# Conv-out products moved to the end of a merge stage, conv taps spread over ten attention rounds, and eight modulation chunks computed on VectorE

## The chip, the cores and the metric

The kernel runs on one NeuronCore of a Trainium2 chip. The metric is the device time of one execution in microseconds (us); of the kernel before it is the median of three runs. The trace quoted here is of one further execution taken by the hardware profiler.

The engines are named as in the profile: PE is TensorE (PEld its weight loads), DVE is VectorE, ACT is ScalarE, POOL is GpSimd, and SP is SyncE, which here only issues DMAs. PEclk is the clock granted to TensorE as a share of full speed: 1.00 is its upper level, 0.50 its lower one.

## What is computed

Two transformer blocks on 512 tokens of width 1024, in float32. The change lies in the first block:

```python
mod = silu(c) @ ada_w + ada_b                       # 1024 -> 6 x 1024: sh1 sc1 ga1 sh2 sc2 ga2
h = rmsnorm(x, pre_mix_g) * (1 + sc1) + sh1
glu_in, qkv, gates = split(h @ w_in)
u = silu(layernorm(depthwise_conv31(u_val * sigmoid(u_gate))))
y_conv = u @ w_conv_out                             # "cout"
y_att = stick_breaking_attention(q, k, v) @ w_att_out   # 8 heads; "aout"
merged = sigmoid(g_conv) * y_conv + sigmoid(g_att) * y_att
y = merged @ w_o                                    # "wo"
x = x + ga1 * rmsnorm(y, post_mix_g)                # needs ga1
h = rmsnorm(x, pre_ffn_g) * (1 + sc2) + sh2         # needs sc2, sh2: the second modulation
x = x + ga2 * rmsnorm(swiglu_ffn(h), post_ffn_g)
```

The second block (retention, latent attention, a conv feed-forward) is not touched.

## The kernel before

**Products.** Every float32 product is done as three float32r products (`mm3`, lines 202 to 204) of split operands: hi x hi, lo x hi, hi x lo. A weight slab of 512 KB is loaded by SP into a `w_st` buffer (a ring of 2), cast by ACT into `w_hi` (line 184), and its remainder is computed into `w_lo` by DVE or POOL (line 207); `w_hi` and `w_lo` have four buffers each. `slab()` takes the next slab of the fixed list `ORDER` and issues slabs ahead.

**Order.** The program is written in one order, and a planner in the framework orders the queue of each engine: it gives each instruction a due time by its own costs, and where several are ready it takes the one that is earliest in the program. On the chip each engine then follows its queue in order. Buffers of one tag are handed out in the order of the program: a tile waits until the tile that is as many back as the tag has buffers is released.

**PSUM.** There are eight banks: two in `psT` (given out by `pt()`, tile `ps_t`), four in `psP` (`pp()`, tile `ps_p`), two in `psC` (tile `ps_c`). The conv accumulators hold `psC` until the taps are done; then `Banks.both` is set and `pp()` uses `psC` as well.

**Attention rounds.** `pipeline` runs ten rounds, t = 0 to 9. In round t head t computes scores and the scan (lines 712 to 723), head t-1 transposes its weights (228), head t-2 multiplies by v (679) and combines (702). `stick_between(t)` then adds the fillers of `STICK_FILL`: q and k products, gate products (16 tiles of 24 products), and before the change `cout` 0 and 1. `step(conv, n)` advances the generator `conv_all` by n parts: fifteen parts of two taps of each of the four channel tiles (three on DVE, line 523; the fourth by ACT and POOL, lines 526 and 527), a last tap with the layer norm of the first token tile, three more layer norms, and the transposes back with SiLU. Three parts are advanced before round 0.

**Modulation chunks.** `ada_acc` computes one chunk of 256 columns of `mod`: two half tiles `ad` of 512 KB each are loaded (line 360). On PE it is sixteen short matmuls (line 385) and a DVE copy (390). On DVE (`ADA.vector`) it is one multiply (376) and seven multiply-adds (378) into the single buffer `acc`. Either way a small PE product over `acc` follows, in a `psT` bank: line 396 for the sc2/sh2 columns (`ada_cols`, then DVE 400 and 403), line 416 for a quarter of the row of ga1 (`ga_row`, then DVE 417 and 418 into `grow`). In the merge the pool `mtmp` has two `ad` buffers, which are the two halves of one chunk, and one `acc` buffer.

**Merge.** For p = 0 to 3: the two remaining conv gates (p >= 2) and `cout` p, then `aout` p; DVE multiplies by the gates (lines 772 and 847), POOL adds (848), ACT casts and DVE subtracts into `mh` and `ml_` (849, 850). Chunks 0 to 5 of the second modulation are done on PE in rounds 3 to 8; chunks 6 and 7 and the four rows of ga1 on DVE in the merge.

**After the merge** the `wo` product runs through `gemm_tok` with eight slabs: four are streamed over all four token tiles, four are resident. The accumulators of its first token tile are the two `psT` banks, those of the others `pp()` banks. `boundary` then updates x with `grow1` (line 331) and makes the next h.

Of the kernel before, what the change touches and what calls it, by code (L numbers as in the profile page):

```python
# [8 lines left out]
F32 = mybir.dt.float32  # L9
# [9 lines left out]
S = 512  # L19
KB = 8  # L20
# [29 lines left out]
for _n, _k in VEC:  # L50
# [6 lines left out]
ORDER = (  # L57
    [("glu", k) for k in range(8)]
    + [("win", 3), ("win", 7)]
    + [("v", i) for i in range(4)]  # L60
)
def _fill(spec):
    return tuple(
        [({"q": "q", "k": "k", "g": "gate", "c": "cout"}[x[0]], int(x[1:])) for x in r.split()] for r in spec.split("|")
    )


STICK_FILL = _fill("q1 k1|g8|q2 k2|g9|q3 k3|g10 g11|g12 g13|g14 g15|g0 g1 c0|g2 g3 c1")
WIN_OF = {"q": 8, "k": 12}
ORDER += [("win", 8), ("win", 12)]  # L70
for _f in STICK_FILL:
    ORDER += [("win", WIN_OF[n] + m) if n in WIN_OF else (n, m) for n, m in _f]
for _p in range(4):
    if _p >= 2:
        ORDER += [("gate", 2 * _p), ("gate", 2 * _p + 1), ("cout", _p)]
    ORDER += [("aout", _p)]
ORDER += [("wo", k) for k in range(8)]
for _m in range(NF):
    ORDER += [("fin", _m), ("fin", NF + _m)]
# [16 lines left out]
def build(tc, nc, a):  # L96
# [38 lines left out]
    def pp():  # L135
        Banks.at = (Banks.at + 1) % 6
        if Banks.both and Banks.at % 3 == 0:
            return conv_bank()
        ps_p = psP.tile([128, 512], F32, tag="p", name="ps_p")
        return ps_p  # L140
# [23 lines left out]
    def vcol(name, i):  # L164
        o = VOFF[name] + i
        return vec[:, o:o + 1]
# [26 lines left out]
    def slab(key, ahead=2):  # L193
        assert ORDER[W.got] == key, (ORDER[W.got], key)
        W.got += 1
        if W.nxt < W.got:
            emit_slab()
        prefetch(ahead)
        return W.ready.pop(key)
# [16 lines left out]
    def mtile(ps, w, rh, rl, nk, width, c0=0, t0=0, t1=S):  # L216
        wh, wl = w
        for k in range(nk):
            c = k * width + c0
            mm3(  # L220
                ps[:, t0:t1], wh[:, c:c + 128], wl[:, c:c + 128],
                rh[:, k, t0:t1], rl[:, k, t0:t1], k == 0, k == nk - 1,
            )
# [128 lines left out]
    class ADA:  # L352
        pool, tag, bufs, nacc = ring, "st", NST, 1
# [10 lines left out]
    def ada_acc(chunk, ap_):  # L364

        ads = ADA.loaded.pop(chunk, None) or ada_load(chunk)
        if ADA.vector:  # L370
            acc = ap_.tile([128, 256], F32, tag="acc", name="acc", bufs=ADA.nacc)
            for hf, ad in enumerate(ads):
                for b in range(4):
                    cc = cact[:, 4 * hf + b, 0:1]
                    if hf == 0 and b == 0:
                        nc.vector.tensor_scalar(out=acc, in0=ad[:, b, :], scalar1=cc, scalar2=None, op0=ALU.mult)
                    else:
                        nc.vector.scalar_tensor_tensor(
                            out=acc, in0=ad[:, b, :], scalar=cc, in1=acc, op0=ALU.mult, op1=ALU.add
                        )  # L380
            return acc, pt()[:, 256:512]
        ps = pt()
        for hf, ad in enumerate(ads):
            for b in range(4):
                nc.tensor.matmul(  # L385
                    out=ps[32 * b:32 * b + 32, 0:256], lhsT=cact[:, 4 * hf + b, :], rhs=ad[:, b, :],
                    start=hf == 0, stop=hf == 1,
                )
        acc = ap_.tile([128, 256], F32, tag="acc", name="acc", bufs=ADA.nacc)
        nc.vector.tensor_copy(acc, ps[:, 0:256])  # L390
        return acc, ps[:, 256:512]

    def ada_cols(i, kb, g_name, ap_):
        acc, ps = ada_acc(8 * i + kb, ap_)
        for s in range(2):
            nc.tensor.matmul(
                out=ps[:, s:s + 1], lhsT=acc[:, s * 128:(s + 1) * 128], rhs=ones[:, 0:1], start=True, stop=True
            )
        sh, sc = 24 * i + kb, 24 * i + 8 + kb
        nc.vector.tensor_tensor(  # L400
            out=modB[:, i, kb:kb + 1], in0=ps[:, 0:1], in1=vcol("ada_b", sh), op=ALU.add
        )
        nc.vector.scalar_tensor_tensor(
            out=modA[:, i, kb:kb + 1], in0=ps[:, 1:2], scalar=vcol("ada_b", sc), in1=vcol(g_name, kb),
            op0=ALU.add, op1=ALU.mult,
        )

    def ga_row(i, grow, ap_, q, gp=None):
        cs = slice(q * 256, (q + 1) * 256)
        gr = (gp or ap_).tile([128, 2, 256], F32, tag="gr", name="gr", bufs=1)  # L410
        for j in range(2):
            nc.sync.dma_start(
                out=gr[:, j, :], in_=a["rows"][2 * i + j:2 * i + j + 1, cs].broadcast_to([128, 256])
            )
        acc, ps = ada_acc(16 + 4 * i + q, ap_)
        nc.tensor.matmul(out=ps[:, 0:256], lhsT=ones, rhs=acc, start=True, stop=True)
        nc.vector.tensor_tensor(out=grow[:, cs], in0=ps[:, 0:256], in1=gr[:, 1, :], op=ALU.add)
        nc.vector.scalar_tensor_tensor(
            out=grow[:, cs], in0=grow[:, cs], scalar=32.0, in1=gr[:, 0, :], op0=ALU.mult, op1=ALU.mult
        )  # L420
# [12 lines left out]
    accp = endp  # L433
# [54 lines left out]
    for kb in range(KB):  # L488
# [3 lines left out]
        n = S // (2 if kb == 0 else 1)  # L492
# [95 lines left out]
    gate = pp()  # L588
# [4 lines left out]
    conv = conv_all()  # L593

    def step(g, n=1):
        for _ in range(n):
            next(g, None)
# [153 lines left out]
    def qk_tile(n, p):  # L751
        ps = pp()
        mtile(ps, slab(("win", WIN_OF[n] + p)), hh, hl, KB, 128)
        if n == "q":
            qk[p] = (evac_stat(ps, qkp),)
        else:
            qk[p] += evac_mov(ps, qkp, kz[p % 2])

    gcs = {}

    def conv_gate(m, sg):
        g = gate_tile(m)
        nc.scalar.activation(out=sg, in_=g, func=AF.Sigmoid)
        gcs[m] = sg

    def conv_out(p):
        cw = slab(("cout", p))
        for j in range(2):
            yc = pp()
            mtile(yc, cw, u2["h"], u2["l"], 4, 256, c0=128 * j)  # L770
            sg = gcs[2 * p + j]
            nc.vector.tensor_tensor(out=sg, in0=sg, in1=yc, op=ALU.mult)

    def early_gate(m):
        st = qkp.tile([128, S], F32R, tag=("st0", "st1", "kz00", "mv0")[m], name="st", bufs=1 if m == 2 else 2)
        return st.bitcast(F32)

    def att_gate(m):
        g = gate_tile(m)
        nc.scalar.activation(out=gat[:, m - 8, :], in_=g, func=AF.Sigmoid)  # L780

    def stick_between(t):
        for n, m in STICK_FILL[t]:
            if n == "gate" and m >= 8:
                att_gate(m)
            elif n == "gate":
                conv_gate(m, early_gate(m))
            elif n == "cout":
                conv_out(m)
            else:  # L790
                qk_tile(n, m)
            step(conv, 1)
        step(conv, (30 if t == 7 else 1))
        for kb in range(KB):
            if AD[kb] == t:
                ada_cols(1, kb, "pre_ffn_g", accp)
        if t in (4, 6, 8):
            split_o(t // 2 - 2)

    AD = (3, 4, 5, 6, 7, 8, 20, 21)  # L800
    ofs, oh, ol = {}, [], []

    def split_o(p):
# [27 lines left out]
    mtmp, mt_s = pool("mtmp", 4)  # L831
    grow_p, _gs = pool("growp", side="right")
    ADA.pool, ADA.tag, ADA.bufs, ADA.vector = mtmp, "ad", 2, True
    grow1 = grow_p.tile([128, D], F32)
    for p in range(4):
        if p >= 2:
            for j in range(2):
                sg = mtmp.tile([128, S], F32, tag="sg", name="sg", bufs=2)
                conv_gate(2 * p + j, sg)
            conv_out(p)  # L840
        gs = [gcs[2 * p], gcs[2 * p + 1]]
        aw = slab(("aout", p))
        for j in range(2):
            m = 2 * p + j
            ya = pp()
            mtile(ya, aw, Tiles(oh), Tiles(ol), 4, 256, c0=128 * j)
            nc.vector.tensor_tensor(out=gat[:, m, :], in0=gat[:, m, :], in1=ya, op=ALU.mult)
            nc.gpsimd.tensor_tensor(out=gs[j], in0=gs[j], in1=gat[:, m, :], op=ALU.add)
            nc.scalar.copy(mh[:, m, :], gs[j])
            lo_of(ml_[:, m, :], gs[j], mh[:, m, :])  # L850
        for kb in range(KB):
            if AD[kb] == 20 + p:
                ada_cols(1, kb, "pre_ffn_g", accp)
        for q in ((0,), (1, 2), (3,), ())[p]:
            ga_row(0, grow1, accp, q, mtmp)
    ADA.pool, ADA.tag, ADA.bufs = ring, "st", NST
    close(mt_s, endp_s)

# [50 lines left out]
    g1 = g_operand(gf, gpool)  # L909
# [394 lines left out]
    g2 = g_operand(gf, gpool)  # L1304
# [147 lines left out]
```

## Time and profile before

| | |
|---|---|
| three runs | median 1402.76 us (1401.82 to 1402.99) |
| the profiled execution | 1402.35 us, of which the span from first to last instruction is 1400.6 us |
| mean granted clock of TensorE | 0.990 |
| PE, DVE, ACT, POOL busy | 96%, 55%, 41%, 24% of the span |
| attention rounds, first scores to the last product by v | 115.7 to 268.7 us |
| merge, to the first `wo` product | to 341.5 us |
| `wo` product | 341.5 to 385.5 us |

Matmuls are pipelined: the trace shows 0.39 us for one of 512 columns, but in a run of them one starts every 0.23 us. A waiting time in brackets is the idle time of the engine just before the instruction, with what ended it.

### The profile page before, as it was taken

To read this page: it belongs to the slowest core of one execution; us is meant where nothing else is said; L and a number is where in the kernel's file an instruction comes from. 1 tells how busy PE (TensorE), PEld (TensorE's weight loads), DVE (VectorE), ACT (ScalarE), POOL (GpSimd) and SP (SyncE) were. 2 spreads that over 40 slices of the span, in tenths; PEclk is the share of its full clock that TensorE was granted. 3 is DMA by queue.
4 is the path that set the end of the run, shared out by engine and by line. 5 is a ranking of instruction groups with operands and counts; after the bars stand their busy time and mean duration, and the time that the engine had idled before them with its cause. 6 is when DMAs were issued, how large, how long until landed. Compare 5 with 4: busy or idle time off the path is not lost.

```text
span 1400.6 us, 17393 instructions
## 1 busy us (share of the span) xinstructions
PE 1348.2 (96%) x6686; PEld 1119.8 (80%) x6686; DVE 769.5 (55%) x1203; ACT 581.2 (41%) x953; POOL 334.7 (24%) x337
## 2 busy tenths in 40 slices
PE   6998999999979999999999999999999999999997
PEld 4786787888878888888887788887888888888886
DVE  3399968477356434323334665788257555554334
ACT  4357655332244322222323526777246433333323
POOL 2279855411150000000002534567020000000000
PEclk9998999999989999999999999999999999999999
DMA  8422133566224334433322322011323332323231
GB/s 323 154 76 88 35 120 120 166 200 197 99 68 141 126 125 128 135 91 94 102 91 93 121 91 92 30 33 46 111 86 120 99 98 93 103 91 105 91 97 69
DMA packets 44578, 152.18 MB, mean 109 GB/s; under 512 B 4912, under 2 KB 7344, under 8 KB 44496
## 3 DMA queue, kind: packets, MB, share of 16 engines
q1 hardware_dynamic: 43008, 146.03, 32.4%
q0 software_dynamic: 1344, 4.84, 0.9%
q8 instruction: 52, 0.85, 0.2%
q14 instruction: 30, 0.25, 0.1%
q10 hardware_dynamic: 144, 0.21, 0.0%
HBM read 146.86 MB, written 4.19 MB: 108 GB/s over the span
## 4 chain that ended last, share of the span: by engine, by line
PE 84%; DVE 7%; ACT 3%; issue 2%; POOL 2%; DMA 1%; SPq 0%; POOLq 0%; ACTq 0%; DVEq 0%
PE ps_p L202 17%; PE ps_p L204 16%; PE ps_p L203 16%; PE ps_c L203 8%; PE ps_c L204 8%; PE ps_c L202 7%; PE ps_t L202 2%; PE ps_t L204 2%; PE ps_t L203 2%; PE ps_t L228 2%; DVE kp L719 1%; PE ps_t L679 1%; DVE ps_c L523 1%; PE ps_t L385 1%; DVE w_lo L207 1%
## 5 line engine op out<-in xcount | busy, mean ns | idle before, releaser
L184 ACT CAST w_hi<-w_st 128x1024 fp32r<-128x1024 f32 (+2 forms) x217 | 225.1, 1040 | 386.1 <-PE ps_p L203 138.7
L207 DVE TENSOR_TENSOR w_lo<-w_st,w_hi 128x1024 fp32r<-128x1024 f32 (+2 forms) x179 | 222.4, 1244 | 235.5 <-ACT w_hi L184 233.8
L203 PE MATMUL ps_p<-hl,w_hi 128*128 128x512 f32 (+1 forms) x740 | 279.6, 379 | 0.4 <-POOL hl L207 0.4
L204 PE MATMUL ps_p<-hh,w_lo 128*128 128x512 f32 (+1 forms) x740 | 278.0, 377 | 1.4 <-DVE w_lo L207 1.4
L202 PE MATMUL ps_p<-hh,w_hi 128*128 128x512 f32 (+1 forms) x740 | 276.5, 382 | 1.9 <-ACT hh L263 1.2
L239 POOL TENSOR_TENSOR r<-q,mhalf 128x1 f32<-128x1 f32 x36 | 20.9, 583 | 764.5 <-DVE q L235 716.7
L202 PEld LDWEIGHTS ps_p<-hh,w_hi 128*128 128x128 f32 x740 | 139.2, 191 | 29.9 <-ACT hh L263 2.5
L204 PEld LDWEIGHTS ps_p<-hh,w_lo 128*128 128x128 f32 x740 | 140.9, 190 | 27.4 <-DVE w_lo L207 2.5
L203 PEld LDWEIGHTS ps_p<-hl,w_hi 128*128 128x128 f32 x740 | 141.1, 191 | 25.8 <-POOL hl L207 1.6
L202 PE MATMUL ps_c<-hh,w_hi 128*128 128x512 f32 (+1 forms) x354 | 130.0, 367 | 3.9 <-ACT hh L263 3.1
L203 PE MATMUL ps_c<-hl,w_hi 128*128 128x512 f32 (+1 forms) x354 | 130.8, 370 | 0.4 <-POOL hl L207 0.4
L204 PE MATMUL ps_c<-hh,w_lo 128*128 128x512 f32 (+1 forms) x354 | 128.8, 364 | 0.0
L207 POOL TENSOR_TENSOR w_lo<-w_st,w_hi 128x1024 fp32r<-128x1024 f32 (+1 forms) x38 | 93.8, 2474 | 57.2 <-ACT w_hi L184 49.0
L207 DVE TENSOR_TENSOR gl<-gf,gh 128x512 fp32r<-128x512 f32 x44 | 30.4, 690 | 105.6 <-ACT gh L899 105.6
L899 ACT CAST gh<-gf 128x512 fp32r<-128x512 f32 x44 | 27.4, 622 | 133.4 <-PE ps_p L203 124.1
L202 PEld LDWEIGHTS ps_c<-hh,w_hi 128*128 128x128 f32 x354 | 67.6, 191 | 15.3 <-ACT hh L263 3.3
L203 PEld LDWEIGHTS ps_c<-hl,w_hi 128*128 128x128 f32 x354 | 67.2, 190 | 10.9 <-POOL hl L207 0.6
L204 PEld LDWEIGHTS ps_c<-hh,w_lo 128*128 128x128 f32 x354 | 67.5, 191 | 10.2
L204 PE MATMUL ps_p<-w_hi,gl 128*128 128x512 f32 x176 | 68.6, 390 | 0.0
L203 PE MATMUL ps_p<-w_lo,gh 128*128 128x512 f32 x176 | 68.5, 389 | 0.0
L202 PE MATMUL ps_p<-w_hi,gh 128*128 128x512 f32 x176 | 68.5, 389 | 0.0
L523 DVE SCALAR_TENSOR_TENSOR ps_c<-upad,vec,ps_c 128x512 f32<-128x512 f32 x87 | 60.6, 747 | 0.7
(428 smaller groups left out, 2564.3 us busy)
## 6 DMA issues: line engine op xcount, KB each, us to landing
ad<-in_ada SPq DMA_DIRECT2D x48, 512.0 KB, 4.1
w_st<-in_w_fin SPq DMA_DIRECT2D x44, 512.0 KB, 3.7
w_st<-in_w_up SPq DMA_DIRECT2D x44, 512.0 KB, 3.4
w_st<-in_w_win SPq DMA_DIRECT2D x22, 512.0 KB, 3.6
w_st<-in_w_fout SPq DMA_DIRECT2D x22, 512.0 KB, 3.5
w_st<-in_w_down SPq DMA_DIRECT2D x22, 512.0 KB, 3.5
w_st<-in_w_gate SPq DMA_DIRECT2D x16, 512.0 KB, 3.7
w_st<-in_w_wo SPq DMA_DIRECT2D x16, 512.0 KB, 3.8
```

Source lines behind the costliest of these rows:

```text
L184: nc.scalar.copy(w_hi[:, :n], w_st[:, :n])
L202: nc.tensor.matmul(out=out, lhsT=lh, rhs=rh, start=start, stop=False)
L203: nc.tensor.matmul(out=out, lhsT=lh, rhs=rl, start=False, stop=False)
L204: nc.tensor.matmul(out=out, lhsT=ll, rhs=rh, start=False, stop=stop)
L207: (eng or nc.vector).tensor_tensor(out=out, in0=src, in1=hi.bitcast(F32), op=ALU.subtract)
L228: nc.tensor.transpose(out=ps[:r, j * 128:(j + 1) * 128], in_=s, identity=ident)
L239: nc.gpsimd.tensor_tensor(out=r, in0=q, in1=mhalf[:, 0:1], op=ALU.pow)
L385: nc.tensor.matmul(out=ps[32 * b:32 * b + 32, 0:256], lhsT=cact[:, 4 * hf + b, :], rhs=ad[:, b, :], start=hf == 0, stop=hf == 1,)
L523: nc.vector.scalar_tensor_tensor(out=out, in0=src, scalar=w, in1=acc, op0=ALU.mult, op1=ALU.add)
L679: nc.tensor.matmul(out=ps[:, kb * 128:S], lhsT=vt(kb, h), rhs=a_slice(at[j], kb, 0, n), start=first, stop=kb == NT - 1 and j == 0,)
L719: nc.vector.tensor_tensor_scan(out=kp[:, :n][:, ::-1], data0=kp[:, :n][:, ::-1], data1=zero.broadcast_to([128, n]), initial=1.0, op0=ALU.m ...
L899: nc.scalar.copy(gh, gf[:, k, :])
```

## The change

`cout` 0 and 1 leave the last two rounds. The merge becomes two loops: first gates and `aout` for all p, each with two chunks of the second modulation, then for all p `cout`, the sum, the cast and one row of ga1. No chunk of the second modulation is left in the rounds; all eight are done by DVE. The conv parts are advanced by one per round and one more in odd rounds, with the rest after round 9. `sg` gets four buffers instead of two.

```diff
-STICK_FILL = _fill("q1 k1|g8|q2 k2|g9|q3 k3|g10 g11|g12 g13|g14 g15|g0 g1 c0|g2 g3 c1")
+STICK_FILL = _fill("q1 k1|g8|q2 k2|g9|q3 k3|g10 g11|g12 g13|g14 g15|g0 g1|g2 g3")
...
     if _p >= 2:
-        ORDER += [("gate", 2 * _p), ("gate", 2 * _p + 1), ("cout", _p)]
+        ORDER += [("gate", 2 * _p), ("gate", 2 * _p + 1)]
     ORDER += [("aout", _p)]
+ORDER += [("cout", _p) for _p in range(4)]
...
-            elif n == "cout":
-                conv_out(m)
             else:
                 qk_tile(n, m)
-            step(conv, 1)
-        step(conv, (30 if t == 7 else 1))
-        for kb in range(KB):
-            if AD[kb] == t:
-                ada_cols(1, kb, "pre_ffn_g", accp)
+            if n == STICK_FILL[t][0][0] and m == STICK_FILL[t][0][1]:
+                step(conv, 1)
+        step(conv, 30 if t == 9 else t % 2)
...
-    AD = (3, 4, 5, 6, 7, 8, 20, 21)
...
-                sg = mtmp.tile([128, S], F32, tag="sg", name="sg", bufs=2)
+                sg = mtmp.tile([128, S], F32, tag="sg", name="sg", bufs=4)
                 conv_gate(2 * p + j, sg)
-            conv_out(p)
-        gs = [gcs[2 * p], gcs[2 * p + 1]]
         aw = slab(("aout", p))
         for j in range(2):
             m = 2 * p + j
             ya = pp()
             mtile(ya, aw, Tiles(oh), Tiles(ol), 4, 256, c0=128 * j)
             nc.vector.tensor_tensor(out=gat[:, m, :], in0=gat[:, m, :], in1=ya, op=ALU.mult)
+        for kb in (2 * p, 2 * p + 1):
+            ada_cols(1, kb, "pre_ffn_g", accp)
+    for p in range(4):
+        conv_out(p)
+        gs = [gcs[2 * p], gcs[2 * p + 1]]
+        for j in range(2):
+            m = 2 * p + j
             nc.gpsimd.tensor_tensor(out=gs[j], in0=gs[j], in1=gat[:, m, :], op=ALU.add)
             nc.scalar.copy(mh[:, m, :], gs[j])
             lo_of(ml_[:, m, :], gs[j], mh[:, m, :])
-        for kb in range(KB):
-            if AD[kb] == 20 + p:
-                ada_cols(1, kb, "pre_ffn_g", accp)
-        for q in ((0,), (1, 2), (3,), ())[p]:
-            ga_row(0, grow1, accp, q, mtmp)
+        ga_row(0, grow1, accp, p, mtmp)
```

## Rows read from the trace of the kernel before

**Rows 1.** The page: busy time of each engine, and the chain by engine

```profile
PE 1348.2 (96%) x6686; PEld 1119.8 (80%) x6686; DVE 769.5 (55%) x1203; ACT 581.2 (41%) x953; POOL 334.7 (24%) x337
...
PE 84%; DVE 7%; ACT 3%; issue 2%; POOL 2%; DMA 1%; SPq 0%; POOLq 0%; ACTq 0%; DVEq 0%
```

**Rows 2.** Windows of the rounds: busy us and instructions, PEclk, DMA share, GB/s

```profile
120.00:130.00 10.00, 10.00 (x38) 8.05 (x37) 9.82 (x12) 5.98 (x10) 9.37 (x8) 0.81 0.01 4
130.00:140.00 10.00, 7.52 (x37) 6.26 (x36) 9.76 (x16) 8.57 (x17) 9.18 (x8) 0.87 0.34 91
```

**Rows 3.** Chain of waits in order of time, rounds 0 to 3: start, us, what

```profile
150.27 3.60 DVE kp L719 x2
```

**Rows 4.** Waits of PE, 60 to 380 us: us in total, times, longest

```profile
PE ps_p L712 <- ACT sp L718: 2.9, 2, 2.5
PE ps_p L712 <- ACT mv L645: 2.1, 1, 2.1
...
PE ps_t L228 <- DVE modA L403: 1.4, 1, 1.4
```

**Rows 5.** Timeline of PE: a chunk of the second modulation in round 4

```profile
190.37 1.07 PE L385 MATMUL ps_t<-ad,cact 128*32 128x256 f32 x16
191.37 0.33 PE L712 MATMUL ps_p<-mv,st 128*128 128x128 f32 x1
```

**Rows 6.** Timeline of PE: chunk products in the merge, and the start of `wo`

```profile
290.15 0.50 PE L396 MATMUL ps_t<-ones,acc 128*128 128x1 f32 x4
...
305.16 0.59 PE L416 MATMUL ps_t<-acc,ones 128*128 128x256 f32 x2
...
341.52 0.39 PE L202 MATMUL ps_c<-w_hi,mh 128*128 128x512 f32 x1
...
352.87 0.59 PE L416 MATMUL ps_t<-acc,ones 128*128 128x256 f32 x2
353.12 0.58 PE L202 MATMUL ps_t<-w_hi,mh 128*128 128x512 f32 x1
```

**Rows 7.** Timeline of SP: loads of chunk halves in the merge

```profile
268.68 0.80 SPq L360 DMA_DIRECT2D ad<-in_ada  x2
```

**Rows 8.** Timeline of DVE: one chunk in the merge, first and last entries

```profile
317.25 0.76 DVE L376 TENSOR_SCALAR acc<-ad,cact 128x256 f32<-128x256 f32 x1
...
324.25 1.00 DVE L378 SCALAR_TENSOR_TENSOR acc<-ad,cact,acc 128x256 f32<-128x256 f32 x2
```

**Rows 9.** Line 360, merge: time of its loads; DVE timeline, a late half chunk

```profile
DMA to landing us min/median/max: 3.5/4.3/6.0
...
575.24 2.05 DVE L378 SCALAR_TENSOR_TENSOR acc<-ad,cact,acc 128x256 f32<-128x256 f32 x4 [3.50 <-DMA ad<-in_ada]
```

**Rows 10.** Windows: the merge's middle; from the last `av` to `wo`; `wo`

```profile
290.00:340.00 50.00, 50.00 (x226) 41.43 (x225) 40.60 (x67) 14.88 (x19) 9.59 (x7) 1.00 0.59 194
268.68:341.52 72.84, 72.84 (x328) 60.35 (x327) 55.84 (x85) 22.98 (x30) 17.85 (x10) 1.00 0.63 207
341.52:385.50 43.98, 43.98 (x197) 36.37 (x195) 19.05 (x29) 11.45 (x18) 6.98 (x6) 1.00 0.36 114
```

**Rows 11.** Timeline of ACT during `wo`: the cast of the fifth slab

```profile
359.21 2.01 ACT L184 CAST w_hi<-w_st 128x1024 fp32r<-128x1024 f32 x2 [12.87 <-PE ps_t L204]
```

**Rows 12.** Windows behind `wo`, where PE has been idle

```profile
390.00:392.00 2.00, 0.00 (x0) 0.00 (x0) 1.40 (x2) 0.77 (x1) 0.52 (x1) 0.50 0.89 349
...
398.00:400.00 2.00, 2.00 (x12) 2.00 (x11) 1.80 (x3) 0.00 (x0) 0.92 (x3) 0.50 0.64 242
```

**Rows 13.** Timeline of DVE: the last part of `grow`, and its first reader

```profile
353.96 0.42 DVE L418 SCALAR_TENSOR_TENSOR grow<-grow,gr 128x256 f32<-128x256 f32 x1
...
375.59 1.41 DVE L331 SCALAR_TENSOR_TENSOR y<-ps_t,r,grow 128x512 f32<-128x512 f32 x2 [0.66 <-POOL r L239]
```

**Rows 14.** Timeline of PE, rounds 4 to 5: four transposes of the layer norm

```profile
200.07 0.60 PE L228 MATMUL ps_p<-identr,cacc 128*128 128x128 f32 x4
200.43 0.48 PE L202 MATMUL ps_p<-hh,w_hi 128*128 128x512 f32 x1
```

## The prediction

> **What bounds the kernel now.** I read the page first. PE is busy 96% of the span and carries 84% of the chain that ended last [rows 1], so a change pays only if it takes work, idle time or a low clock from PE, and costs only where PE comes to wait. Next the windows of the stage that is edited. In rounds 0 to 3 PE is not the limit: DVE is busy 9.8 of 10 us at 120 to 140, while PE loses 2.5 us at 130 to 140 and its clock is granted at 0.81 and 0.87, a mix of its two levels [rows 2]. The chain there runs through DVE: scans (line 719) between the conv multiply-adds (line 523) [rows 3]. The list of PE's waits shows what is lost: 2.9 us for the sigmoids that free score banks, 2.1 us for the first k operand, and one 1.4 us wait for a modulation column (403), which holds a `psT` bank [rows 4]. From round 4 to the end of `wo` PE has hardly a gap: it is busy 72.84 of 72.84 us from the last product by v to `wo`, and 43.98 of 43.98 us in `wo` [rows 10].
>
> Then I followed the chunks through the merge, because the change doubles their number there. What the reader is to see is a second chain beside PE, hidden so far. The small products that end the chunks stand on PE at 290.15 (chunk 6), 305.16 and 352.87, with three more between the last two: the pace is (352.87 - 305.16) / 4 = 11.9 us a chunk [rows 6]. By the program chunk 6 and all four rows are due by the third `aout`, which PE finishes around 319; the last comes 34 us later. So the chunks are not placed by the program; they are as late as their own chain makes them. One `acc` buffer and two `ad` buffers allow one chunk at a time: a half is loaded again only after its four operations.
>
> And PE does wait for this chain's end by a tie that is easy to miss: the `psT` banks. The first token tile of `wo` accumulates in `psT`, and banks are handed out in program order, so it cannot begin before the last chunk's product has its bank. It shows: `wo` begins at 341.52 in `ps_c` and `ps_p`, and the first `wo` product into `ps_t` is at 353.12, directly behind the last chunk at 352.87 [rows 6]. Until then PE lives on the other three token tiles of the slabs already there; the cast of the fifth slab waits 12.87 us until a `ps_t` product frees a buffer [rows 11]. The row of ga1 itself is not what is late: it is done at 354.4 and first read at 375.59 [rows 13].
>
> **The change, part by part.**
>
> *Chunks 0 to 5 leave PE.* One costs 1.0 us of PE (190.37 to 191.37) [rows 5]: 6 x 1.0 = -6.0 us. The column products (396) stay. The wait of 1.4 us goes with them [rows 4]: -1.4.
>
> *Taps spread over the rounds.* The same 93 DVE taps and 31 ACT/POOL pairs remain; later in the program they yield to scans that are ready. DVE then stops being the limit in rounds 0 to 3. At most it gives back PE's waits for ACT there, 2.9 + 2.1 us [rows 4], and what the clock falls short of 1.00 in two windows, 10 x (0.19 + 0.13) = 3.2 us [rows 2]: 8.2 us. At least nothing, because taps run ahead wherever DVE is free, and the wait for the k operand is not made by DVE. I take half, -4. Against it, the conv accumulators now hold the two `psC` banks until round 8 instead of round 4, so rounds 4 to 8 run on four banks; the waits on banks with four, 2.9 + 2.1 us in four rounds [rows 4], are the bound for five more rounds: 0 to +6, and since DVE is less loaded then I take +2. PE's gain before the merge: 6.0 + 1.4 + 4 - 2 = 9.4 us (bounds 6.0 + 1.4 - 6 = 1 and 6.0 + 1.4 + 8.2 = 16).
>
> *`cout` 0 and 1 and the layer norm move behind the rounds.* PE's work is unchanged. A product costs 43.98 / 192 = 0.229 us [rows 10]; `cout` 0, 24 products, moves from before the last product by v to behind it: 5.5 us. (`cout` 1 is behind it already.) The layer norm's 32 transposes, 0.36 us for four [rows 14], add 2.9. The fillers they were in the last rounds are not missed if gates 0 to 3 (22 us of products) cover the last head: I cost that at nothing, and at up to 3 us if they don't.
>
> *Twelve chunks in a row on DVE.* The chain starts where its buffers come free, at the last product by v, as now: first load at 268.68, first column product at 290.15, 21.5 us later [rows 6, 7]. From there to `wo` PE has 72.8 us of work now [rows 10], then 72.8 + 5.5 + 2.9 = 81.2 us. In `wo` it can do three of four token tiles of four slabs, 4 x 18 x 0.229 = 16.5 us, before it must have `psT`. So PE reaches the wall 97.7 us after the chain's start. The chunks done by then are 1 + (97.7 - 21.5) / 11.9 = 7.4 of 12. Behind the wall PE and DVE have nothing else, so a chunk costs its own chain only: the load of the second half after its buffer is free, 4.3 us, and its four multiply-adds, 2.05 us [rows 9], with the small product 6.5 us. A chunk takes 8.0 us on DVE in the merge (317.25 to 325.25) [rows 8], so the eighth, begun some 5 us before the wall, needs 3 more, and four more cost 26: PE stands still for 29 us.
>
> The pace is the disputed number. Its bounds are 6.5 us (the chain alone; no stall worth speaking of) and 15.0 us (the slowest interval, 290.15 to 305.16 [rows 6]; 6.1 done, stall 37 us). I take the 11.9 of the same stage, same buffers and same neighbours. DVE cannot do much better anyhow: it is busy 40.6 of 50 us in the merge [rows 10], of which some 20 us are chunks (4.3 of them at 8 operations of about 0.5 and a tail), so other work needs 41%; on 81.2 us that is 33, plus four gate multiplies and two `w_lo` (5 us) and the conv's norm and SiLU (about 9 us). The 34 us left hold 7 to 8 chunks at 4.5.
>
> *Restart.* After an idle stretch PE is granted 0.50, the lower level of 1.2 GHz, from 390 to 400 before it is back at the upper one [rows 12]. Ten us at half rate with some 6.7 busy cost 3.3; I take +2 for the first products behind the wall (0 to 4).
>
> *`sg` with four buffers, sums and casts at the end.* The last `mh` is needed at the eighth slab only, 20 us into `wo`: nothing. Work behind the wall is the same as before.
>
> **Sum**, against the profiled 1402.35 us (span 1400.6 and 1.75 around it): -9.4 + 29 + 2 = +21.6, so 1424.0; the median of the runs is 0.4 above the profiled time. I say 1424. A difference of 0.2%, 2.8 us, is about what a measurement of this kernel can tell from none.
>
> **Rivals.**
>
> A, the chunks keep pace, and the change is faster. For it: a chunk's own chain is 6.5 us, and what paces it now is partly the planner's due times, which run late: the chunk that ends at 325.25 on DVE [rows 8] has its product on PE only some 3 us later. It decides at a pace where the stall is smaller than the gain: 9.4 us of stall are 1.4 chunks, so 10.6 of 12 done by the wall, 76.2 / 9.6 = 7.9 us. Against it: no interval of rows 6 is below 11, and DVE has no room. Time: 1402.4 - 9.4 = 1393, up to 1399 with a chunk of stall left.
> The Trainium skill, Perfetto Trace Analysis, section "Identifying the Most-Contended Engine", says to optimise first the engine with the highest occupancy. By that rule alone, work that goes from a PE at 96% to a DVE at 55% [rows 1] is a gain, and rival A is its result. The trace speaks for the rule in the rounds and against it in the merge, where DVE is at 81% [rows 10].
>
> B, gain and stall cancel: pace near 9, or DVE more relieved in the rounds. 1400 to 1407.
>
> C, DVE falls so far behind in the merge that `w_lo` of a slab comes late and PE waits inside the merge as well. The slabs are two ahead, 11 us of PE, so it decides where DVE lags more than that. It adds about 10: 1433 to 1450.
>
> **How the numbers follow.** The forecast 0.69, from 1407 (gain 16, pace 10, no restart cost: 8.6 done, stall 21) to 1442 (gain 1, stall 37, restart 4: +40); A 0.17; B 0.08; C 0.06. Faster is A with 0.17, same is B with 0.07, slower is the rest with 0.76. The range from 1394 to 1442 leaves out half of A, half of C and a little of the forecast.
>
> **What would show it.** Right: a PE gap of 20 us or more about 16 us after the first `wo` product, ended by DVE (378 or 418), with the last chunk's product directly before the first `ps_t` product of `wo`; eight products of line 396, then four of 416, about 12 us apart up to the wall and 6 to 8 behind it; DVE over 85% busy in the merge; no line 385 in the rounds; fewer PE waits on 718 at 115 to 150. Wrong: chunks 8 us apart or less, `wo` products into `ps_t` from its start, or `wo` given other banks by the planner's order. The sizes least sure are the pace and the relief of rounds 0 to 3.

## The result, and the profile after

| | before | after |
|---|---|---|
| runs | 1402.9 us (1401.8 to 1403.1) | 1442.4 us (1442.0 to 1442.9) |
| ratio, 95% interval | 1 | 1.0281 (1.0269 to 1.0294) |
| profiled execution, its span | 1402.35, 1400.6 us | 1442.85, 1441.1 us |
| mean granted clock | 0.990 | 0.973 |

The change makes the kernel 2.8% slower, 39.5 us: the forecast's direction, but 18 us more than its 1424 and 0.4 us above the top of its range. Lines of the file lie one lower in the kernel after (a chunk's column product is L397, its row product L417, its loads L361).

First the page of the kernel after: busy time, and the chain by engine, to be read against [rows 1].

```profile
PE 1349.0 (94%) x6590; PEld 1121.6 (78%) x6590; DVE 782.2 (54%) x1247; ACT 581.2 (40%) x953; POOL 329.9 (23%) x335
...
PE 80%; DVE 9%; ACT 3%; DMA 3%; issue 2%; POOL 2%; SPq 0%; POOLq 0%; DVEq 0%; ACTq 0%
```

The 96 matmuls of six chunks are gone, and yet PE is busy no shorter: some of its work ran at the lower clock. DMA is on the chain with 3% instead of 1%: loads have become part of the path.

PE's timeline, kernel after, the entries that answer to [rows 6]: start, us, what, and in brackets the idle time ahead of it.

```profile
303.06 0.50 PE L397 MATMUL ps_t<-ones,acc 128*128 128x1 f32 x4
...
334.73 0.39 PE L203 MATMUL ps_c<-w_hi,mh 128*128 128x512 f32 x1
...
349.44 0.50 PE L397 MATMUL ps_t<-ones,acc 128*128 128x1 f32 x4
354.60 1.01 PE L397 MATMUL ps_t<-ones,acc 128*128 128x1 f32 x4 [2.22 <-DVE acc L379]
360.61 1.01 PE L397 MATMUL ps_t<-ones,acc 128*128 128x1 f32 x4 [5.00 <-DVE acc L379]
...
391.77 1.22 PE L417 MATMUL ps_t<-acc,ones 128*128 128x256 f32 x2 [5.21 <-DVE acc L379]
392.43 0.99 PE L203 MATMUL ps_t<-w_hi,mh 128*128 128x512 f32 x1
```

`wo` begins 6.8 us earlier than before (341.52), but its first product into `ps_t` comes at 392.43 instead of 353.12, directly behind the last of twelve chunks. Five chunks are done at 349.44, (349.44 - 303.06) / 4 = 11.6 us apart; the other seven come behind the wall, (391.77 - 354.60) / 6 = 6.2 us apart. The same in windows of the kernel after (columns as in [rows 2]): the last product by v to `wo`, `wo` up to the wall, the standstill, the rest of `wo`.

```profile
251.15:334.73 83.58, 80.75 (x377) 66.90 (x377) 56.48 (x88) 26.40 (x35) 18.53 (x14) 1.00 0.44 140
334.73:351.80 17.07, 17.07 (x80) 14.08 (x79) 14.51 (x27) 2.48 (x4) 3.88 (x2) 1.00 0.50 162
351.80:392.43 40.63, 7.94 (x24) 5.00 (x22) 27.24 (x65) 0.00 (x0) 0.00 (x0) 0.53 0.59 183
392.43:421.00 28.57, 28.57 (x122) 23.50 (x121) 9.22 (x14) 9.27 (x16) 3.17 (x4) 0.95 0.38 135
```

In 40.6 us PE works 7.9, at a granted clock of 0.53, close to its lower level; ACT and POOL do nothing, since no buffer of the slabs comes free. ACT's timeline, kernel after, has the cast of the fifth slab, to be read against [rows 11]:

```profile
397.59 2.01 ACT L185 CAST w_hi<-w_st 128x1024 fp32r<-128x1024 f32 x2 [54.46 <-PE ps_t L205]
```

Before, `wo` had no gap at all [rows 10]. DVE is not the limit ahead of `wo`: it is busy 56.48 of 83.58 us, 68%, where over 85% was expected. PE's waits in the kernel after, 60 to 440 us, to be read against [rows 4]:

```profile
PE ps_t L417 <- DVE acc L379: 20.7, 4, 5.7
PE ps_t L397 <- DVE acc L379: 12.0, 3, 5.0
PE ps_t L229 <- DVE xn L253: 6.3, 1, 6.3
PE ps_p L713 <- ACT sp L719: 4.4, 4, 2.7
PE ps_c L229 <- DVE upad L560: 2.8, 1, 2.8
```

The first two are the chunks. The wait for `upad`, the layer norm that now stands behind the rounds, is new; that for `xn`, behind `wo`, was 3.3 us before; the waits for the sigmoids of the rounds are not fewer.

What was not foreseen shows on SP. Its timeline, kernel after, against [rows 7]:

```profile
281.58 0.33 SPq L184 DMA_DIRECT2D w_st<-in_w_aout  x1
286.56 0.33 SPq L184 DMA_DIRECT2D w_st<-in_w_cout  x1
286.94 1.86 SPq L361 DMA_DIRECT2D ad<-in_ada  x2
```

The first chunk of the merge is loaded at 286.94, 36 us behind the last product by v (251.15), and on the queue behind all slab loads up to the first `cout`. On DVE the last multiply of the conv's SiLU starts at 286.45, 0.5 us before that load:

```profile
286.45 0.68 DVE L579 TENSOR_TENSOR u<-u,s 128x512 f32<-128x512 f32 x1
```

And the first token tile of `wo` is read by DVE 38 us later than in [rows 13]:

```profile
413.97 1.41 DVE L332 SCALAR_TENSOR_TENSOR y<-ps_t,r,grow 128x512 f32<-128x512 f32 x2 [0.66 <-POOL r L240]
```

### The profile page after: what moved, and what is told of

It is laid out like the page before. It is cut to its first block, busy times and chain, and to the rows that moved or that the text cites. A ratio compares the mean times of both kernels' runs of the same rounds, so it can differ in the third digit from the quotient of the medians.

```text
span 1441.1 us, 17259 instructions
## 1 busy us (share of the span) xinstructions
PE 1349.0 (94%) x6590; PEld 1121.6 (78%) x6590; DVE 782.2 (54%) x1247; ACT 581.2 (40%) x953; POOL 329.9 (23%) x335
## 4 chain that ended last, share of the span: by engine, by line
PE 80%; DVE 9%; ACT 3%; DMA 3%; issue 2%; POOL 2%; SPq 0%; POOLq 0%; DVEq 0%; ACTq 0%
PE ps_p L203 16%; PE ps_p L204 16%; PE ps_p L205 16%; PE ps_c L204 7%; PE ps_c L203 7%; PE ps_c L205 7%; DMA ad<-in_ada 2%; PE ps_t L229 2%; PE ps_t L203 2%; DVE acc L379 2%; PE ps_t L204 2%; PE ps_t L205 2%; DVE w_lo L208 1%; PE ps_t L680 1%; ACT w_hi L185 1%
## 5 line engine op out<-in xcount | busy, mean ns | idle before, releaser
L204 PE MATMUL ps_c<-hl,w_hi 128*128 128x512 f32 (+1 forms) x346 | 127.8, 370 | 1.6 <-POOL hl L208 1.6
L203 PE MATMUL ps_c<-hh,w_hi 128*128 128x512 f32 (+1 forms) x346 | 126.5, 366 | 1.9 <-ACT w_hi L185 0.9
L205 PE MATMUL ps_c<-hh,w_lo 128*128 128x512 f32 (+1 forms) x346 | 125.3, 362 | 0.0
L208 POOL TENSOR_TENSOR w_lo<-w_st,w_hi 128x1024 fp32r<-128x1024 f32 (+1 forms) x36 | 87.1, 2422 | 65.8 <-ACT w_hi L185 57.7
L379 DVE SCALAR_TENSOR_TENSOR acc<-ad,cact,acc 128x256 f32<-128x256 f32 x112 | 58.0, 518 | 18.7 <-DMA ad<-in_ada 15.9
```

What stands on the lines that cost most here:

```text
L203: nc.tensor.matmul(out=out, lhsT=lh, rhs=rh, start=start, stop=False)
L204: nc.tensor.matmul(out=out, lhsT=lh, rhs=rl, start=False, stop=False)
L205: nc.tensor.matmul(out=out, lhsT=ll, rhs=rh, start=False, stop=stop)
L208: (eng or nc.vector).tensor_tensor(out=out, in0=src, in1=hi.bitcast(F32), op=ALU.subtract)
L379: nc.vector.scalar_tensor_tensor(out=acc, in0=ad[:, b, :], scalar=cc, in1=acc, op0=ALU.mult, op1=ALU.add)
```

## The experiments

The theory: the merge pool `mtmp` has grown from 14 to 18 KB a partition (four `sg`, two `ad`, `gr`), more than the 16 KB that v leaves, so it lies over temporaries of the conv, which now ends 36 us behind the last product by v; the chunk loads are queued behind that. Rivals: the moved products, the spread taps, or DVE itself cost the time. All times below are medians, with the ratio to the kernel before on the same chip. On the chips of these runs the kernel before takes 1401.9 to 1403.6 us.

### The sigmoids outside the merge pool

```diff
-                sg = mtmp.tile([128, S], F32, tag="sg", name="sg", bufs=4)
-                conv_gate(2 * p + j, sg)
+                tag = ("st1", "mv0", "kz10", "kz11")[2 * p + j - 4]
+                sg = qkp.tile([128, S], F32R, tag=tag, name="sg", bufs=2 if p == 2 else 1)
+                conv_gate(2 * p + j, sg.bitcast(F32))
```

> The kernel after, with the four sigmoid tiles of conv gates 4 to 7 taken from free tiles of the attention's operand pool, so that the merge's own pool is 10 KB instead of 18. Theory: the chunk chain began 36 us after the last product by v (first load at 286.9 instead of about 251) because an 18 KB pool reaches past the 16 KB of v into the memory of the conv's temporaries, and the planner holds the whole pool until the conv's SiLU is done. Then the first load goes out near 251, the first column product comes near 272, and by the wall at 352 some 1 + 80 / 11.6 = 7.9 chunks are done; the stall falls from 40.7 to about 25 us and the time to about 1426 us. Rival: the load is late because it stands behind weight slabs in the program's order; then nothing moves, 1442 us.

1423.6 us, ratio 1.0158 (1.0143 to 1.0173): 21.7 us above the kernel before on its chip instead of 39.5, so 17.8 gone. SP's timeline of this run has the first load 0.3 us behind the last product by v (249.13):

```profile
249.44 0.80 SPq L361 DMA_DIRECT2D ad<-in_ada  x2
```

The products stand 12.4 us apart ((347.89 - 261.12) / 7), eight chunks are done at 347.89, and the first `ps_t` product of `wo` comes at 374.77. The late start is 18 us of the loss.

### The conv parts advanced as before, the pool as it is

```diff
-            if n == STICK_FILL[t][0][0] and m == STICK_FILL[t][0][1]:
-                step(conv, 1)
-        step(conv, 30 if t == 9 else t % 2)
+            step(conv, 1)
+        step(conv, 30 if t == 7 else 1)
```

> The kernel after, with nothing but the advance of the conv parts as in the kernel before: one part for each filler and one more per round, the rest after round 7. The merge pool keeps its four sg buffers, so it still lies over the conv's temporaries. Theory: the first chunk load came 36 us late because those temporaries were in use until the conv's SiLU; with the conv done in round 8 the first load comes at the last product by v (about 250), its first product about 12 us later, 8 chunks are done at the wall, and the 2.8 us wait for the layer norm behind round 9 goes: 1418 to 1424 us. If rounds 0 to 3 do lose the relief that spread taps were to give, the last product by v comes up to 4 us later. Rival: the size of the pool alone delays it, whenever the conv ends: the first load stays near 287 and the time at 1440 or above.

1424.9 us, 1.0153 (1.0140 to 1.0167), 0.9 us above the expected range and 21.8 above the kernel before. SP's first merge load here, with the 18 KB pool (last product by v at 253.80):

```profile
254.10 0.81 SPq L361 DMA_DIRECT2D ad<-in_ada  x2
```

So it takes both, the large pool and the late conv, to hold the loads back; either repair gives the same 18 us. (In the run with two accumulators below, the pool is 16 KB and the conv late: its first load goes out at 250.59, with the last product by v.) Without spread taps `wo` also starts earlier, at 332.51 instead of 334.73: the spread costs 2.2 us there, where I had it gain. PE's timeline of this run at the wall:

```profile
332.51 0.39 PE L203 MATMUL ps_c<-w_hi,mh 128*128 128x512 f32 x1
...
373.66 1.22 PE L417 MATMUL ps_t<-acc,ones 128*128 128x256 f32 x2 [4.88 <-DVE acc L379]
374.32 0.99 PE L203 MATMUL ps_t<-w_hi,mh 128*128 128x512 f32 x1
```

Against the run with the sigmoids outside, `wo` starts 3.8 us earlier, the first `ps_t` product comes 0.45 us earlier, and the spans are 0.6 us apart (1421.1 and 1421.7): an earlier `wo` is worth nothing while the chunks are late.

### Three half-chunk buffers

The first experiment's edit, and:

```diff
-    ADA.pool, ADA.tag, ADA.bufs, ADA.vector = mtmp, "ad", 2, True
+    ADA.pool, ADA.tag, ADA.bufs, ADA.vector = mtmp, "ad", 3, True
```

> The kernel of e1 with three buffers for chunk halves instead of two (14 KB). Theory: the pace of 11.6 us in the merge and of 6.2 us behind the wall is set by the second half, which is loaded only after its buffer is used up. With a third buffer the pace behind the wall falls to about 5 us (eight operations, 3.9 us, and the small product) and in the merge to 8 to 9 us; 10 to 11 chunks are done by the wall, the stall is under 10 us and the time 1400 to 1409 us. Rival: DVE's other work sets the pace in the merge; then it stays near 11.6 and the time is that of e1 less 5 us.

1422.9 us, 1.0145 (1.0128 to 1.0162), no different from 1423.6: a miss of the expected 1400 to 1409. The pace of the merge stays at 12.4 us; behind the wall it falls to some 5.6. The load of the second half doesn't pace the merge.

### Two accumulators

The edit above, and both chunk calls take `acc` from the merge pool, with two buffers:

```diff
-    ADA.pool, ADA.tag, ADA.bufs, ADA.vector = mtmp, "ad", 3, True
+    ADA.pool, ADA.tag, ADA.bufs, ADA.vector, ADA.nacc = mtmp, "ad", 3, True, 2
...
-            ada_cols(1, kb, "pre_ffn_g", accp)
+            ada_cols(1, kb, "pre_ffn_g", mtmp)
...
-        ga_row(0, grow1, accp, p, mtmp)
+        ga_row(0, grow1, mtmp, p, mtmp)
```

> The kernel after with the sigmoids of gates 4 to 7 outside the merge pool, three chunk-half buffers (as in the run with three halves, 1422.9 us) and two acc buffers instead of one. Theory: the pace of 12.4 us in the merge is set by the single acc: the next chunk's first DVE operation waits until PE has run the small product of the chunk before, which stands 2 to 4 us behind in PE's queue, and what DVE does in between is other work. With two the interval falls to 9 or 10 us, 10 to 11 of the 12 chunks are done when wo reaches the psT banks, and the time is 1404 to 1412 us. Rival: the pace is set by DVE's other work and the order of its queue; then the interval stays above 11.5 us and the time within 4 us of 1423.

1408.8 us, 1.0043 (1.0030 to 1.0057), as expected and 14 us better (15 by the distances to the kernel before). The last chunk is at 357.57 instead of 371.69: on the mean (357.57 - 262.27) / 11 = 8.7 us a chunk. The single `acc` did pace the merge. In the run without `sg` in the pool a chunk's last multiply-add starts at 283.61, its product stands on PE only at 288.25, and the next chunk's first multiply comes at 289.41. That run's DVE timeline, then its PE timeline:

```profile
283.61 0.47 DVE L379 SCALAR_TENSOR_TENSOR acc<-ad,cact,acc 128x256 f32<-128x256 f32 x1
...
289.41 0.34 DVE L377 TENSOR_SCALAR acc<-ad,cact 128x256 f32<-128x256 f32 x1
```

```profile
288.25 0.50 PE L397 MATMUL ps_t<-ones,acc 128*128 128x1 f32 x4
```

DVE had room for the faster chain: with two accumulators it is busy 79.16 of the 92.12 us from the last product by v to `wo`, 86%. One product was queued too early here, and PE stood still for it (PE's timeline, two accumulators):

```profile
269.00 1.02 PE L397 MATMUL ps_t<-ones,acc 128*128 128x1 f32 x4 [5.51 <-DVE acc L379]
```

### No row chunks

`ga_row` leaves out its chunk and product; `grow` is built from the loaded rows alone:

```diff
-        ga_row(0, grow1, accp, p, mtmp)
...
+        nc.vector.scalar_tensor_tensor(
+            out=grow1[:, cs], in0=gr[:, 1, :], scalar=32.0, in1=gr[:, 0, :], op0=ALU.mult, op1=ALU.mult
+        )
```

> The kernel after without the four row chunks: the row of ga1 is made from the bias and the gain alone, so four of twelve chunks are left out, and nothing that the update of x reads is late. Theory: the first token tile of wo waits for its PSUM bank behind the last chunk in the program, whatever that chunk is for; then the eight column chunks alone still stall wo until the eighth product, about 4 x 6.2 = 25 us earlier than now: stall 15 us, 1417 us. Rival: PE waits because the row of ga1 is needed; then no stall is left and the time is about 1400 us, since the columns are read only after wo.

1416.9 us, 1.0110 (1.0095 to 1.0125). PE's timeline, the last column chunk and `wo` into `ps_t`:

```profile
366.98 1.01 PE L397 MATMUL ps_t<-ones,acc 128*128 128x1 f32 x4 [5.15 <-DVE acc L379]
367.86 0.77 PE L203 MATMUL ps_t<-w_hi,mh 128*128 128x512 f32 x1
```

`wo` needs neither sc2 nor sh2, and still its first token tile waits for the last of these chunks. The wait is for the bank, as predicted, not for ga1.

### Six chunks back on PE, twice

Chunks 0 to 5 as before in rounds 3 to 8, the rest of the change kept; the second run with the first experiment's edit too:

```diff
+        if 3 <= t <= 8:
+            ada_cols(1, t - 3, "pre_ffn_g", accp)
...
-        for kb in (2 * p, 2 * p + 1):
-            ada_cols(1, kb, "pre_ffn_g", accp)
+        if p < 2:
+            ada_cols(1, 6 + p, "pre_ffn_g", accp)
```

> The kernel after with chunks 0 to 5 back on TensorE in rounds 3 to 8; taps spread, conv-out at the end and the large pool as they are. Six chunks are left in the merge. Theory: the loss is the chain of chunks and nothing else. The first product comes about 16 us after the conv's SiLU, near 309, and five more at 11.6 us end near 367, against a wall near 358: stall about 5 us, 1402 to 1410 us. Rival: the loss comes from the spread taps and the moved conv-out products; then it stays above 1425 us.

> The kernel after with chunks 0 to 5 back on PE in rounds 3 to 8 and with the sigmoids of gates 4 to 7 outside the merge pool, so that the first merge load is not late. Against the run with only the conv-out products moved (1401.3 us) it differs in the spread of the taps, with the layer norm and the SiLU behind round 9. Theory: of the 17.6 us between six chunks on PE (1418.9 us) and that run, the late chunk load makes about 5 us and the spread taps the rest, so 1410 to 1416 us. Rival: all of it is the late load and what hangs on it; then 1401 to 1405 us.

1418.9 (1.0120, 1.0105 to 1.0135) and 1418.7 us (1.0113, 1.0099 to 1.0126). The first was expected at 1402 to 1410, a miss. That expectation priced only the time that PE stands still for chunks, which is 3.5 us here; but the first `ps_t` product of `wo` comes at 368.58, 15.5 us later than before, and the first y with it. The second misses its 1410 to 1416 and its rival's 1401 to 1405. In it the first merge load comes 31 us earlier, at 267.29 instead of 298.67, and nothing is won: two of the chunks get done early, then a gap of 30 us follows (products at 303.26 and 333.00), and the last stands at 370.18. In this change a row chunk comes behind each `cout` in the program, and seemingly so in the queues. PE's timeline of the second run and its window from 270 to 280:

```profile
280.25 0.47 PE L229 MATMUL ps_c<-identr,upad 128*128 128x128 f32 x1 [6.75 <-DVE upad L560]
```

```profile
270.00:280.00 10.00, 3.50 (x24) 2.93 (x22) 8.14 (x17) 2.69 (x3) 1.48 (x3) 0.86 0.79 282
```

Here PE waits 6.8 us outright for the layer norm behind the rounds, while DVE is shared by taps, norm and the first chunk.

### Only the conv-out products moved

The kernel before, with `cout`, sums and casts moved as in the change, four `sg`; taps, chunks and rows as before.

```diff
+ORDER += [("cout", _p) for _p in range(4)]
...
+    for p in range(4):
+        conv_out(p)
+        gs = [gcs[2 * p], gcs[2 * p + 1]]
```

> The kernel before, with only the conv-out products, the sums and the casts moved to the end of the merge (sg with four buffers); taps and the chunks on PE in rounds 3 to 8 as before. It is the run with six chunks on PE (1418.9 us) less the spread of the taps and less the layer norm behind round 9. Theory: the move alone costs nothing that matters, 1401 to 1405 us, and the 16 us of that run are the spread taps and what they push behind the rounds. Rival: the moved products are the cost, because the rounds lose 48 products as fillers and all sums and casts end late: 1410 us or more.

1401.3 us, 0.9986 (0.9977 to 0.9995): the move costs nothing, as predicted. The 18 us up to the two runs above thus lie in what still differs, the spread taps and the place of the row chunks, which no run tells apart: `wo` starts at 350.24 in the second of them against 342.09 here, and its first `ps_t` product comes 20.3 us behind that start instead of 6.0.

### DVE chunks in the rounds

The kernel before with one line, so that chunks 0 to 5 are multiply-adds where they stood:

```diff
+    ADA.vector = True
     strict = mask_tile(apool, 0)
```

> The kernel before, with only this changed: chunks 0 to 5 stay in rounds 3 to 8 but are done as DVE multiply-adds instead of sixteen short PE matmuls. Theory: the loss of the change lies in where the chunks stand, behind round 9 and ahead of a bank that wo needs, and not in their being on DVE; in rounds 4 to 8 DVE has room, PE is spared 6 us, and the time is 1395 to 1400 us. Rival: with DVE at 9.8 of 10 us in rounds 0 to 3 and the psT banks shared with the transposes of the rounds, a chunk that ends late holds up a transpose, as it does the first token tile of wo; then PE waits in the rounds and the time is 1403 to 1412 us.

1416.4 us, 1.0098 (1.0083 to 1.0114): the rival, and above its 1403 to 1412. From 160 to 280 PE is busy 106.5 us against 117.9 before, at a clock of 0.96 against 1.00, and DVE 92.4 against 79.7. PE's waits of this run, 100 to 360:

```profile
PE ps_t L396 <- DVE al L207: 5.5, 2, 3.1
PE ps_t L228 <- DVE of L702: 3.2, 2, 2.7
```

The 5.5 us are two waits for a chunk's own product: it stands in PE's queue before the chunk is ready. DVE's timeline ahead of the longer one, and the product on PE:

```profile
257.02 0.47 DVE L378 SCALAR_TENSOR_TENSOR acc<-ad,cact,acc 128x256 f32<-128x256 f32 x1
257.41 0.55 DVE L207 TENSOR_TENSOR al<-ps_t,ah 128x384 fp32r<-128x384 f32 x1
```

```profile
258.01 0.61 PE L396 MATMUL ps_t<-ones,acc 128*128 128x1 f32 x4 [3.06 <-DVE al L207]
```

The chunk's last multiply-add ends at 257.49, late in the wait of 3.06 us; `al`, which reads a `psT` bank, adds the last 0.5 us. The 3.2 us are transposes that wait for `of`, attention work of DVE that the multiply-adds share the engine with. In the rounds a DVE chunk costs more than it spares.

### Fewer chunks on PE, with the repairs

Conv parts as before, two `acc`, three halves, `sg` outside, and four or two chunks on PE, in rounds 3 to 6 or 3 and 4. With two:

```diff
+        if 3 <= t < 5:
+            ada_cols(1, t - 3, "pre_ffn_g", accp)
...
-        for kb in (2 * p, 2 * p + 1):
+        for kb in range(KB)[2 + 2 * p:4 + 2 * p]:
```

> What the runs point to, put together: conv-out products at the end of the merge, taps as in the kernel before, two acc buffers, three chunk-half buffers, the sigmoids outside the pool, and four chunks on PE in rounds 3 to 6 instead of six; eight on DVE in the merge. Theory: PE is spared 2 us and the 1.4 us wait, the move of the conv-out products gives 1.5 us as measured, and eight chunks at the 8.7 us of the run with two acc buffers are done well ahead of the psT banks: 1396 to 1400 us, faster than both kernels. Rival: chunk products queued early make PE wait, as the 5.5 us in the run with two acc buffers: 1402 to 1407 us.

> As the run with four chunks on PE, with two on PE in rounds 3 and 4 and ten on DVE in the merge. Theory: ten chunks need about 12 + 9 x 8.7 = 90 us from the last product by v, PE reaches the psT banks after about 95, so there is no long stall and the time is 1396 to 1402 us. Rival: DVE cannot keep 8.7 us beside the conversions late in the merge; two or three chunks are left at the banks and the time is 1405 to 1412 us.

1404.7 us with four on PE, 1.0013 (1.0004 to 1.0022): a miss, though not by the wait that I had as the rival. Its first `ps_t` product comes 1.5 us earlier than before and yet the first y does not (375.70 against 375.59); why is open. 1399.7 us with two, 0.9977 (0.9968 to 0.9986). `wo` starts at 339.50 and 336.69: two chunks off PE are worth 2.8 us, 1.4 each. The last row chunk stands at 351.30 and 348.49, well after `wo` has begun.

### The rows ahead of the conv-out loop

```diff
+    for p in range(4):
+        ga_row(0, grow1, mtmp, p, mtmp)
     for p in range(4):
         conv_out(p)
...
-        ga_row(0, grow1, mtmp, p, mtmp)
```

> The run with two chunks on PE and ten on DVE (1399.7 us), with the four row chunks ahead of the conv-out loop in the program instead of one behind each conv-out. Theory from the traces so far: the end of the span follows the first read of the first token tile of wo (372.9 there, 375.6 before, 414.0 after, each some 1025 us ahead of the end), and that tile starts when the last chunk has its bank. In the run with two on PE DVE is only 45% busy from 310 to 320, ahead of the rows; with the rows early the last chunk ends some 8 us sooner, the first token tile starts with wo near 337, and the time is 1394 to 1398 us. Rival: once the last chunk is ahead of wo the other token tiles and the slabs set the end, or the chunks push the conversions of wo's slabs back and wo starts later; then 1399 to 1403 us.

1397.8 us, 0.9961 (0.9947 to 0.9974): faster than both kernels, with ten of the twelve chunks on DVE. A run with all twelve on DVE and the same repairs was not made. PE's timeline: the last chunk is ahead of `wo`, which begins in `ps_t`.

```profile
334.53 0.59 PE L417 MATMUL ps_t<-acc,ones 128*128 128x256 f32 x2
336.72 0.47 PE L203 MATMUL ps_t<-w_hi,mh 128*128 128x512 f32 x1
```

DVE's timeline has its first read, to be held against [rows 13]:

```profile
370.42 1.41 DVE L332 SCALAR_TENSOR_TENSOR y<-ps_t,r,grow 128x512 f32<-128x512 f32 x2 [0.67 <-POOL r L240]
```

All fourteen kernels in one table, in order of the span; the points are start times in each profiled execution.

| kernel | last by v | `wo` starts | last chunk | first `ps_t` of `wo` | first y | span | span - y |
|---|---|---|---|---|---|---|---|
| rows first | 256.1 | 336.7 | 334.5 | 336.7 | 370.4 | 1395.9 | 1025.5 |
| two on PE | 257.2 | 336.7 | 348.5 | 348.8 | 372.9 | 1398.0 | 1025.1 |
| `cout` moved alone | 270.1 | 342.1 | 347.9 | 348.1 | 374.2 | 1399.6 | 1025.4 |
| before | 268.4 | 341.5 | 352.9 | 353.1 | 375.6 | 1400.6 | 1025.0 |
| four on PE | 264.1 | 339.5 | 351.3 | 351.7 | 375.7 | 1402.1 | 1026.4 |
| two `acc` | 250.3 | 342.4 | 357.6 | 361.0 | 381.2 | 1407.3 | 1026.1 |
| DVE in the rounds | 280.1 | 354.6 | 365.9 | 366.2 | 388.7 | 1413.9 | 1025.2 |
| no row chunks | 250.0 | 333.5 | 367.0 | 367.9 | 390.4 | 1414.8 | 1024.4 |
| six on PE, `sg` outside | 265.9 | 350.2 | 370.2 | 370.5 | 391.0 | 1417.2 | 1026.2 |
| six on PE | 265.9 | 346.4 | 367.9 | 368.6 | 391.0 | 1417.3 | 1026.3 |
| conv early | 253.8 | 332.5 | 373.7 | 374.3 | 396.7 | 1421.1 | 1024.4 |
| three halves | 250.2 | 337.4 | 371.7 | 372.4 | 394.8 | 1421.4 | 1026.6 |
| `sg` outside | 249.1 | 336.3 | 374.1 | 374.8 | 396.5 | 1421.7 | 1025.2 |
| after | 251.2 | 334.7 | 391.8 | 392.4 | 414.0 | 1441.1 | 1027.1 |

The reader is to see the last column: from the first y on every kernel needs the same 1024 to 1027 us, and the whole difference is made ahead of it. The start of `wo` says nothing of the time; the last chunk's place says nearly all, down to about 348 us, and less below that.

## Why the prediction was too low

**The step that failed** is "The chain starts where its buffers come free, at the last product by v, as now". The last product by v came where the steps put it: 268.68 - 9.4 - 5.5 - 2.9 = 250.9, measured 251.15. The chain did not start there but at 286.94. I had looked for the buffers in `ad` and `acc` and not for the place of their pool: four `sg` make it larger than the room that v leaves, and the temporaries underneath belong to a conv that the same change makes late. Two edits meet in it, the four `sg` and the spread taps, and neither was costed for the other. By the start alone the wall is reached with five chunks done instead of eight; the two repairs give 17.8 and 17.7 us (39.5 less 21.7 and 21.8, each against the kernel before on its chip), and the miss was 18.4. Which of the planner's rules puts the loads that late, I did not settle: that both conditions are needed is shown, the rule is not.

**What held.** The tie of `wo` to the last chunk by `psT` (no row chunks: the tie goes over to the column chunks). The wall, 17 us into `wo` against 16.5. The pace, 11.6 against 11.9, and 12.4 and 11.4 in the two repair runs, where eight chunks were done at the wall against 7.4. (The way to the first product was shorter than the 21.5 us taken: 16.1 in the kernel after, 11.7 with the sigmoids outside.) The pace behind the wall, 6.2 against 6.5. The moved conv-out products at nothing. The lower clock in the standstill: 0.53.

**What was off in size.** The gain ahead of `wo` was 6.8 instead of 9.4 us. A chunk off PE is worth 1.4 us in the one pair of runs that differs by nothing else, against the 1.2 that I gave it with its share of the wait. The taps are the wrong way round: I had them gain 4 us, less 2 for the banks, and the run with the conv early shows them to cost 2.2 at the start of `wo`. The layer norm behind the rounds is enough for that, a wait of 2.8 us: the sum had "up to 3 us" for the moved fillers and took nothing. DVE in rounds 0 to 3 is as full as in [rows 2]: 9.80 and 9.73 of 10 us. The argument that DVE cannot do much better than the pace was wrong: 27 of the 83.58 us ahead of `wo` are idle on it. The sum also left out that before the change the first `ps_t` product came 11.6 us into `wo`, not 16.5 or more. That product moves by the gain ahead of `wo`, the way into `wo` and the standstill: -6.8 + 5.5 + 40.6 = 39.3 us, of the 39.5 measured. The +2 for the restart does not show there: from that product to the first y it is 21.5 us, against 22.5 before. With the chain's start repaired by the sigmoids outside the pool, the same sum is -5.2 + 5.5 + 21.4 = 21.7 us. That it meets the forecast's 21.6 is luck: the gain was 4.2 us too high there, the standstill 7.6 too long, 5.5 were missing, and the 2 for the restart did not come.

**The rivals.** A, the chunks keep pace, was not met by the change, and its reason against (no interval below 11) was right for one `acc` only: with two, chunks go at 8.7 us. The price named there, 7.9 us, would have been the point to look at: what paced the chain could be changed. C did not come: inside the merge PE waited 2.8 us, for the layer norm and not for `w_lo`. On the Trainium skill's rule (Perfetto Trace Analysis, "Identifying the Most-Contended Engine"), to optimise the engine with the highest occupancy first: the change follows it and loses 2.8%, and the same relief in the rounds loses 1.0%; ten chunks on DVE with an early start, two accumulators and early rows win 0.4%. For TensorE that section goes by the use of its peak and the share of weight loads, not by matmul time; with the loads at 80% against DVE's 55% [rows 1] TensorE is the fuller engine by that as well. The measurements decide here by place, not by occupancy.

## What to carry to other kernels

Hidden work that ends in a shared bank or buffer is a second critical path: find who is next in line for that bank, and make the sum in the start of that one, not in the busy time of the fullest engine. When a change enlarges a pool and makes its neighbour in memory live longer, look at what is loaded into the pool, even if neither edit touches the loads. A single accumulator between two engines paces a chain by the place of its reader in that engine's queue; a second one can be worth more than a third load buffer (14 us here, against nothing clear of noise).

## What the runs showed that was not expected

From the first read of the first `wo` tile to the end, fourteen kernels took 1024.4 to 1027.1 us, though `wo` began anywhere from 332.5 to 354.6 and `ps_t` from 336.7 to 392.4. And starting `ps_t` earlier gives back only part: with the rows first it starts 16.4 us before its time in the kernel before, y only 5.2 us, because the first tile then shares PE with the other three from the beginning (33.7 us from its first product to y, against 22.5).
